# Masked attention over a tree, one core: three stores give their last partitions to SyncE's queue

## The chip, the core and the metric

The kernel runs on one core of a Trainium2 chip. The core has a matrix engine (TensorE, PE in the profile), a vector engine (VectorE, DVE), an activation engine (ScalarE, ACT), GpSimd (POOL) and SyncE (SP), which only issues transfers here. 16 DMA engines, which all queues share, move data between the DRAM and the on-chip memory of 128 partitions. POOL, SP and ACT each have a DMA queue of their own. The metric is the device time of one execution in microseconds (us), the median of several runs; less is better.

## The reference

Q, K and V have 8 x 12 = 96 heads of 512 rows of 64 floats. Row i may look at itself and at its ancestors in a binary tree.

```
mask[i, i] = 1;  parent = i
while parent > 0:
    parent = (parent - 1) // 2
    mask[i, parent] = 1
...
scores = einsum('bhqd,bhkd->bhqk', Q, K) / sqrt(64) + (1 - mask) * (-1e9)
weights = exp(scores - max);  weights = weights / (sum + 1e-10)
out = einsum('bhqk,bhkd->bhqd', weights, V)     # float32, [8, 12, 512, 64]
```

## The kernel before

The heads are taken in 48 pairs, and in twelve groups of eight heads (four pairs, `GP = 4`). The work of a pair has three parts. `T` transposes keys and queries on PE and copies them out of PSUM on DVE. `S` computes two score tiles on PE (lines 489 to 541), the mask as a product of codes that is added to them, and their exponentials on ACT. `V` multiplies with the values on PE (line 552), and `norm` (line 575) takes the reciprocal of the sums on DVE (line 585) and multiplies by it (line 590). The loop at line 767 runs `S T V` for each pair.

Loads are issued by POOL, in groups of eight heads, K, Q and V, and turn float32 into bf16 on the way. POOL also copies values and keys into the layouts that PE reads (lines 306 and 324). What POOL does stands in an order written out by hand, the string `POOL` (line 612): `k`, `q`, `v` are loads, `K`, `Q`, `t`, `c` are copies, `s0` to `s10` are the stores of eight heads, `p44` and `p45` stores of a pair. A word is emitted when `ready` (line 648) allows it; a store `s` of group g waits until pair 4 (g + 1) is due.

The results of groups 0 to 10 are written by `norm` into ten tiles `of` of 128 partitions x 8 heads x 256 floats, 1 MB each; a partition holds 8 x 1 KB of a tile, 8 KB. `of` of group 10 takes the buffer of group 0; the other groups have a buffer to themselves. `store` (line 597) issues one DMA of a whole tile on POOL's queue. The last four pairs have tiles `ol` of 256 KB and are stored by `store_pair` (line 604): pairs 44 and 45 by POOL, pair 46 by SP, pair 47 in two halves by SP and ACT. SP does nothing else from the first microseconds until pair 46 is done.

In the string, `s0` stands behind the last V load, `s1` behind the last K and Q loads, `s2` to `s4` among the copies for the last groups, and from `s5` on nothing but stores is left:

```
"k72 q72 K7 Q7 v80 k80 q80 t4.0 K8 v88 s0 Q8 k88 q88 t4.8 s1 K9 Q9 t5.0 s2 K10 s3 Q10 t5.8 s4 K11 Q11 s5 s6 s7 s8 s9 s10 p44 p45 "
```

Of the kernel before, what the change touches and what calls it, by code (L numbers as in the profile page):

```python
# [11 lines left out]
CODE_ROWS = 40  # L12
CODE_BITS = 16
NOUT = 10
COARSE = range(1, 12)
COARSE_K = range(1, 12)
BESIDE = {"K": range(3, 12), "Q": range(3, 12)}
# [104 lines left out]
def kernel(  # L122
# [7 lines left out]
    nc = tc.nc  # L130
    B, H, S, D = Q.shape
    P = nc.NUM_PARTITIONS
# [5 lines left out]
    KB, VB = 8, 16  # L138
# [13 lines left out]
    Or = out.rearrange("b h (p t) d -> p (b h) (t d)", t=4)  # L152
# [14 lines left out]
    small = ctx.enter_context(tc.tile_pool(name="small", bufs=4))  # L167
    opool = ctx.enter_context(tc.tile_pool(name="opool", bufs=NOUT))
    olast = ctx.enter_context(tc.tile_pool(name="olast", bufs=GP))
# [61 lines left out]
    def head(i, a):  # L231

        g, x = divmod(i, GP)
        return KB * g + GP * a + x if g in COARSE else 2 * i + a

# [13 lines left out]
    qTs, kTs, kqps, obs, ets, ofs = {}, {}, {}, {}, {}, {}  # L249
# [12 lines left out]
    def load_coarse(kept, name, src, h0, n):  # L262

        assert n == KB
        issued.update((name, h) for h in range(h0, h0 + n))
        to = kept[h0 // KB] = loads.tile([P, 2, 16, D], bf16, name=name)
        return nc.gpsimd.dma_start(
            out=to[:, :, :, :].rearrange("p g s d -> p g (s d)"),
            in_=src[32 * h0:32 * (h0 + n), :].rearrange("(g r) c -> r g c", g=2),
        )  # L270
# [6 lines left out]
    def load_q(h0, n):  # L277
        if h0 // KB in COARSE:
            return load_coarse(qsts, "qst", Qc, h0, n)
        return load(qsts, loads, "qst", KB, Qr, h0, n)  # L280
# [29 lines left out]
    def lay_beside(copy, name, g):  # L310
# [4 lines left out]
        src = kept[:, :, :, :].bitcast(mybir.dt.uint32)  # L315
        if g not in COARSE:
            src = src.rearrange("p (x a) t w -> p x t a w", a=2)
        elif name == "Q" or g in COARSE_K:
            src = src.rearrange("p a s w -> p s a w")
        else:  # L320
            src = src.rearrange("p (a x) t w -> p (x t) a w", a=2)
        if g in COARSE:
            dst = dst.rearrange("p x t a w -> p (x t) a w")
# [53 lines left out]
    def transpose_coarse(i):  # L377

        g, x = divmod(i, GP)
        kqps[i] = kqps[i - 1] if x == 3 else psT.tile([P, 2, 32, 32], bf16, name="kqp")  # L380
        if x < 2 and g in COARSE_K:
            assert all(("kst", h) in issued for h in range(KB * g, KB * g + KB))
            return transpose_rows(i, x)
        if x < 2:
            for half in range(2):
                transpose_keys(GP * g + 2 * x + half, kqps[i], half)
            return
        assert all(("qst", h) in issued for h in range(KB * g, KB * g + KB))
        for half in range(2):
            for y, t in enumerate(ORDER):  # L390
                four = 2 * x - 4 + half
                for rows, src in turned(
                    "Q", g, t, lambda b: b[:, four, t, :, :], lambda a: qsts[g][:, a, 4 * four + t, :]
                ):
                    u = 16 * half + y
                    dst = kqps[i][rows, x - 2, u:u + 13:4, :]
                    nc.tensor.transpose(out=dst, in_=src, identity=eye[:, 0:128])  # L397

    def transpose(i, halves=(0, 1)):
        g = i // GP  # L400
        if g in COARSE:
            return transpose_coarse(i)
# [18 lines left out]
    def evac(i):  # L421
# [5 lines left out]
        if g in COARSE_K:  # L427
            dst = kqgs[g][:, 1, 2 * (x % 2):2 * (x % 2) + 2, :, :]
        elif g in COARSE:
            dst = kqgs[g][:, 2 * (x % 2):2 * (x % 2) + 2, x // 2, :, :]  # L430
# [164 lines left out]
            )  # L595

    def store(eng, g):
        return eng.dma_start(  # L598
            out=Or[:, KB * g:KB * g + KB, :],
            in_=ofs[g][:, :, :, :].rearrange("p h t d -> p h (t d)"),  # L600
        )


    def store_pair(eng, i, a=0, n=2):
# [14 lines left out]
    def pool_program():  # L619

        ops = []
        for word in POOL.split():
            kind, *n = word[0], *(int(x) for x in word[1:].split(".") if x)
            if kind in "kqv":
                h0, size = n if len(n) == 2 else (n[0], KB)
                ops.append(({"k": load_k, "q": load_q, "v": load_v}[kind], h0, size))
            elif kind in "KQ":
                ops.append((lay_early if kind == "K" else lay_q, n[0]))
            elif kind == "c":
                o, part, h0, h1 = n  # L630
                ops.append((spread, nc.gpsimd.tensor_copy, o, part, h0, h1))
            elif kind == "t":
                o, h0 = n
                ops += [
                    (spread, nc.gpsimd.tensor_copy, o, part, h0, h0 + KB)
                    for part in (6, 7, 8, 9) + ((), (4, 5))[min(o, 1)]
                ]
            elif kind == "s":
                ops.append((store, nc.gpsimd, n[0]))
            elif kind == "p":  # L640
                ops.append((store_pair, nc.gpsimd, n[0]))
            elif kind == "e":
                ops.append((eye_order,))
            else:
                ops.append((code_order, n[0]))
        return ops
# [162 lines left out]
```

## Time and profile before

| what | value |
|---|---|
| median of 3 runs | 132.43 us (131.93 to 133.2) |
| the profiled execution | 132.84 us |
| its span, first to last instruction | 130.8 us |
| mean granted clock of TensorE | 0.986 |
| busy: PE, DVE, ACT, POOL | 88%, 73%, 76%, 74% |
| read from and written to DRAM | 37.86 MB, 12.58 MB |

The page gives busy times by engine, a strip of 40 equal slices of the span in which a digit is the busy share in tenths, the DMA queues (q0 is POOL's, q1 SP's, q10 ACT's, q8 and q14 fetch instructions) and the chain of work that ended last. A DMA share of 1.0 or more means that the packets of all 16 DMA engines cover the time; they overlap a little. The GB/s count bytes as they are written, so a load that halves its data counts half.

### The profile page before, as it was taken

Reading aid. Unit: us, or ns where it says so; the run is one execution under the profiler, and the core shown is the slowest. Engines: PE = TensorE matmul, PEld = TensorE weight load, DVE = VectorE, ACT = ScalarE, POOL = GpSimd, SP = SyncE. Lnnn points to the kernel's source line nnn. Section 1 sums busy time; section 2 is a strip of 40 time slices with the busy share of each in tenths; the row PEclk is TensorE's granted clock in tenths of the full one; section 3 lists DMA queues with packets and bytes.
Section 4 is the critical chain, followed back from the end, with each engine's and each line's share of the span. In section 5 each row is a group of like instructions: output and inputs, shape, how many; then the busy total and the mean of one; then the engine's idle time right before and its main releaser. Section 6 shows DMA issues by size and latency. Waiting matters only on the chain.

```text
span 130.8 us, 4949 instructions
## 1 busy us (share of the span) xinstructions
PE 115.4 (88%) x2132; PEld 82.6 (63%) x2133; DVE 95.9 (73%) x179; ACT 99.0 (76%) x160; POOL 96.3 (74%) x149
## 2 busy tenths in 40 slices
PE   4989996999998998995999997989989999989930
PEld 1444565776866676774776875767767777856620
DVE  4236778758958959774989798798998898775460
ACT  4339553787988988886778886887897897899920
POOL 6979978239899999999999999999996930202300
PEclk9999999999999999999999999999999999999995
DMA  4999999999999999999999999999999999999992
GB/s 124 195 185 205 209 185 211 201 211 205 210 197 217 201 206 202 209 205 207 212 199 211 202 209 207 205 210 232 336 220 357 406 401 401 401 402 401 384 352 94
DMA packets 24533, 32.13 MB, mean 246 GB/s; under 512 B 944, under 2 KB 15920, under 8 KB 24512
## 3 DMA queue, kind: packets, MB, share of 16 engines
q0 software_dynamic: 23232, 30.67, 110.9%
q1 hardware_dynamic: 720, 0.70, 1.7%
q10 hardware_dynamic: 560, 0.46, 1.0%
q8 instruction: 16, 0.26, 0.7%
q14 instruction: 5, 0.04, 0.1%
HBM read 37.86 MB, written 12.58 MB: 385 GB/s over the span
## 4 chain that ended last, share of the span: by engine, by line
PE 59%; DVE 25%; POOL 6%; issue 3%; ACT 3%; ACTq 0%; POOLq 0%
PE ob L552 16%; DVE kq L436 7%; PE s L494 7%; DVE of L590 7%; PE kqp L375 7%; PE s L499 6%; PE kqp L397 6%; PE s L519 5%; DVE vt L306 5%; PE s L525 5%; PE s L718 3%; POOL vt L306 3%; PE ob L718 2%; PE kqp L350 2%; DVE rec L585 2%
## 5 line engine op out<-in xcount | busy, mean ns | idle before, releaser
L510 ACT ACTIVATE e<-s 128x1024 bf16<-128x1024 f32 x48 | 49.1, 1023 | 21.3 <-PE s L499 20.9
L306 POOL COPY vt<-vst 32x256 uint32<-32x256 uint32 (+2 forms) x70 | 34.9, 499 | 8.9 <-DMA vst<-in_V_dram 5.7
L541 ACT ACTIVATE e<-s 128x384 bf16<-128x384 f32 (+1 forms) x92 | 41.4, 505 | 0.0
L552 PE MATMUL ob<-vt,e 128*128 128x65 bf16 (+1 forms) x940 | 36.9, 197 | 2.4 <-DVE of L590 2.1
L552 PEld LDWEIGHTS <-e 128*128 128x128 bf16 (+1 forms) x960 | 31.2, 102 | 7.9 <-DVE of L590 3.7
L590 DVE TENSOR_TENSOR of<-ob,rec 128x512 f32<-128x512 f32 x44 | 30.4, 691 | 1.5
L306 DVE COPY vt<-vst 32x512 uint32<-32x512 uint32 (+1 forms) x33 | 20.6, 625 | 1.0
L499 PE MATMUL s<-kq 64*128 64x512 bf16 x96 | 18.4, 379 | 2.1 <-DVE kq L436 2.1
L525 PEld LDWEIGHTS <-kq 64*128 64x128 bf16 x384 | 16.3, 110 | 6.3
L598 POOL DMA_DIRECT2D out_dram<-of x11 | 9.8, 897 | 13.5 <-DVE of L590 13.5
L585 DVE RECIPROCAL rec<-ob 128x8 f32<-128x8 f32 x47 | 9.6, 204 | 12.8 <-PE ob L552 12.5
L444 DVE COPY kq<-kqp 128x1024 bf16<-128x1024 bf16 x22 | 15.1, 687 | 4.9 <-PE kqp L375 4.4
L525 PE MATMUL s<-kq 64*128 64x160 bf16 (+1 forms) x384 | 17.9, 210 | 0.0
L494 PE MATMUL s<-qcoarse,codes 40*128 40x512 bf16 x88 | 17.2, 387 | 0.0
L519 PE MATMUL s<-qcoarse,codes 40*128 40x480 bf16 x88 | 16.3, 364 | 0.3
L436 DVE COPY kq<-kqp 128x2048 bf16<-128x2048 bf16 x11 | 13.5, 1224 | 2.2 <-PE kqp L397 1.8
L375 PE MATMUL kqp<-mixed,Kbeside 128*128 128x128 bf16 x144 | 11.1, 220 | 2.8 <-POOL Kbeside L324 1.7
L519 PEld LDWEIGHTS <-codes 40*128 40x128 bf16 x96 | 7.6, 95 | 8.4 <-issue 2.0
L306 ACT COPY vt<-vst 32x512 uint32<-32x512 uint32 (+1 forms) x17 | 10.7, 627 | 1.7 <-DMA vst<-in_V_dram 1.3
L397 PE MATMUL kqp<-ptile,Qbeside 128*128 128x128 bf16 x144 | 11.2, 220 | 0.2 <-DVE kq L444 0.2
L375 PEld LDWEIGHTS <-Kbeside 128*128 128x128 bf16 x144 | 8.3, 98 | 4.2 <-POOL Kbeside L324 2.0
L257 POOL DMA_DIRECT2D vst<-in_V_dram x12 | 10.9, 910 | 0.0
(45 smaller groups left out, 102.2 us busy)
## 6 DMA issues: line engine op xcount, KB each, us to landing
out_dram<-of POOLq DMA_DIRECT2D x11, 1024.0 KB, 15.6
vst<-in_V_dram POOLq DMA_DIRECT2D x12, 512.0 KB, 14.0
kst<-in_K_dram POOLq DMA_DIRECT2D x11, 512.0 KB, 11.9
qst<-in_Q_dram POOLq DMA_DIRECT2D x11, 512.0 KB, 12.3
out_dram<-ol POOLq DMA_DIRECT2D x2, 256.0 KB, 5.3
qst<-in_Q_dram POOLq DMA_DIRECT2D x3, 128.0 KB, 7.1
ol<-in_K_dram SPq DMA_DIRECT2D x1, 256.0 KB, 2.9
ol<-in_Q_dram ACTq DMA_DIRECT2D x1, 256.0 KB, 3.2
```

The source lines that it names most:

```text
L306: return copy(out=dst, in_=src)
L375: nc.tensor.transpose(out=dst, in_=src, identity=perm)
L397: nc.tensor.transpose(out=dst, in_=src, identity=eye[:, 0:128])
L436: return nc.vector.tensor_copy(out=dst, in_=src) if x == 3 else None
L494: nc.tensor.matmul(out=columns(g, sp[:, a, :], 0, 512), lhsT=k1code[64 * a:64 * a + CODE_ROWS, :], rhs=query_codes(i, a, 0, 0, 512), start ...
L499: nc.tensor.matmul(out=columns(g, sp[:, a, :], 0, 512), lhsT=keys(i, a, TOP), rhs=queries(i, a, 0, 512), start=False, stop=True,)
L510: nc.scalar.activation(out=dst, in_=src, func=AF.Exp, scale=scale)
L519: nc.tensor.matmul(out=columns(g, flat[:, a, :], 32, 512), lhsT=k2code[64 * a:64 * a + CODE_ROWS, :], rhs=query_codes(i, a, 1, 32, 512), s ...
L525: nc.tensor.matmul(out=columns(g, flat[:, a, :], lo, hi), lhsT=keys(i, a, TILE2[t]), rhs=queries(i, a, lo, hi), start=False, stop=t == 1,)
L541: nc.scalar.activation(out=dst, in_=src, func=AF.Exp, scale=scale)
L552: nc.tensor.matmul(out=ob[lo:hi, a, 65 * t:65 * t + 65], lhsT=e[:, a, PLACE[t], lo:hi], rhs=vt[:, head(i, a) % VB, tile_v, 0:D + 1], **flags,)
L590: nc.vector.tensor_tensor(out=dst, in0=o4[:, a:a + n, :, 0:D], in1=rec[:, a:a + n, :, :].to_broadcast([P, n, 4, D]), op=ALU.mult,)
```

## The change

`store` cuts the tile of three of the groups by partitions, by a table `SPLIT`. The first piece goes out on POOL's queue, where the whole tile went before; the other pieces go out on SP's queue.

```diff
+SPLIT = {1: (112, 120, 128), 4: (120, 124, 128), 7: (120, 122, 124, 126, 128)}
...
     def store(eng, g):
-        return eng.dma_start(
-            out=Or[:, KB * g:KB * g + KB, :],
-            in_=ofs[g][:, :, :, :].rearrange("p h t d -> p h (t d)"),
-        )
+        cuts = SPLIT.get(g, (P,))
+        for n, (lo, hi) in enumerate(zip((0,) + cuts, cuts)):
+            (nc.sync if n else eng).dma_start(
+                out=Or[lo:hi, KB * g:KB * g + KB, :],
+                in_=ofs[g][lo:hi, :, :, :].rearrange("p h t d -> p h (t d)"),
+            )
```

POOL stores 112 partitions of group 1 and 120 of groups 4 and 7. SP stores 2 x 8 partitions of group 1, 2 x 4 of group 4 and 4 x 2 of group 7. All other stores stay whole. The lines of the kernel move by one to three (`store` issues from line 601, `store_pair` from 610).

SP's program before, whole. `ol` is the tile of a pair, and a wait is given in brackets (DVE's is for the data, DMAHW's for an earlier DMA of SP or ACT that used the same semaphore):

```order
L804 UNCONDITIONAL_BRANCH [waits barrier_Pool_Activation_PE_DVE_SP_release]
L183 DMA ol<-in_K_dram 128x2x256
L191 DMA codes<-tree_codes 16x1280 [waits DVE_49]
L607 DMA out_dram<-ol 128x2x256 [waits DVE_49]
L607 DMA out_dram<-ol 128x256 [waits DVE_49]
L804 UNCONDITIONAL_BRANCH
```

And SP's program now, from the load of the codes to the last store. `of` is the tile of eight heads:

```order
L192 DMA codes<-tree_codes 16x1280 [waits DVE_49]
L601 DMA out_dram<-of 8x8x256 [waits DVE_49]
L601 DMA out_dram<-of 8x8x256
L601 DMA out_dram<-of 4x8x256 [waits DVE_49]
L601 DMA out_dram<-of 4x8x256
L601 DMA out_dram<-of 2x8x256 [waits DMAHW0_49,DVE_49]
L601 DMA out_dram<-of 2x8x256 [waits DMAHW1_49]
L601 DMA out_dram<-of 2x8x256 [waits DMAHW2_49]
L601 DMA out_dram<-of 2x8x256 [waits DMAHW3_49]
L610 DMA out_dram<-ol 128x2x256 [waits DMAHW4_49,DVE_49]
L610 DMA out_dram<-ol 128x256 [waits DMAHW5_49,DVE_49]
```

Eight DMAs have come in between; the first of each group waits for DVE, and none for POOL.

POOL's program before, at its end, from the copy of group 10's keys on:

```order
L324 COPY Kbeside<-kst 128x1024
L598 DMA out_dram<-of 128x8x256
L324 COPY Qbeside<-qst 128x1024
L306 COPY vt_118<-vst 32x8x32 x4
L306 COPY vt_118<-vst 64x8x2x32 x2
L598 DMA out_dram<-of 128x8x256
L324 COPY Kbeside<-kst 128x1024
L324 COPY Qbeside<-qst 128x1024
L598 DMA out_dram<-of 128x8x256 x6
L607 DMA out_dram<-ol 128x2x256 x2
```

And now:

```order
L325 COPY Kbeside<-kst 128x1024
L601 DMA out_dram<-of 128x8x256
L325 COPY Qbeside<-qst 128x1024
L307 COPY vt_118<-vst 32x8x32 x4
L307 COPY vt_118<-vst 64x8x2x32 x2
L601 DMA out_dram<-of 120x8x256
L325 COPY Kbeside<-kst 128x1024
L325 COPY Qbeside<-qst 128x1024
L601 DMA out_dram<-of 128x8x256 x2
L601 DMA out_dram<-of 120x8x256
L601 DMA out_dram<-of 128x8x256 x3
L610 DMA out_dram<-ol 128x2x256 x2
```

No step of POOL has moved; two of the stores shown (of groups 4 and 7), and that of group 1 further up, carry fewer partitions.

## The prediction

> **What bounds the kernel now.** I read the page first for the whole span, then the table by stage for its end, then the chain of waits, then the DMA view in short windows.
>
> ```profile
> span 130.8 us, 4949 instructions
> PE 115.4 (88%) x2132; PEld 82.6 (63%) x2133; DVE 95.9 (73%) x179; ACT 99.0 (76%) x160; POOL 96.3 (74%) x149
> DMA  4999999999999999999999999999999999999992
> q8 instruction: 16, 0.26, 0.7%
> HBM read 37.86 MB, written 12.58 MB: 385 GB/s over the span
> ```
>
> No compute engine is full, but the DMA engines are, in 38 of the 40 slices. The profiled run took 132.84 us, 2.0 more than its span and 0.41 above the median of the three runs (132.43); sums below are made against 132.84 and then moved down by 0.41.
>
> ```profile
> core 0: us, PE busy (x) PEld busy (x) DVE busy (x) ACT busy (x) POOL busy (x), PEclk, DMA share, GB/s
> 106.00:111.00 5.00, 4.96 (x90) 3.58 (x88) 4.43 (x10) 4.39 (x8) 0.00 (x0) 1.00 1.02 401
> 111.00:116.00 5.00, 4.63 (x94) 3.50 (x90) 4.01 (x8) 4.53 (x8) 0.89 (x1) 1.00 1.03 401
> 116.00:121.00 5.00, 4.65 (x92) 3.22 (x93) 2.55 (x7) 4.77 (x9) 0.89 (x1) 1.00 1.02 403
> 126.00:128.20 2.20, 0.00 (x0) 0.00 (x0) 0.80 (x3) 0.00 (x0) 0.00 (x0) 0.75 0.85 313
> 128.20:129.60 1.40, 0.00 (x0) 0.00 (x0) 0.00 (x0) 0.00 (x0) 0.00 (x0) 0.50 0.28 96
> 129.60:130.80 1.20, 0.00 (x0) 0.00 (x0) 0.00 (x0) 0.00 (x0) 0.00 (x0) 0.50 0.00 0
> ...
> 126.41 0.42 DVE ol L590
> ...
> 126.87 0.35 ACTq L607 DMA_DIRECT2D out_dram<-ol  x1
> ```
>
> From 106 us on only stores run (the last load is in by 101.2, a row below), at 401 to 403 GB/s. Compute ends at 126.83 (the last multiply), the last store is issued at 126.87, and then there are 2.7 us in which only DMA runs. The next line is the DMA share in steps of 50 ns from 128.0 to 130.0.
>
> ```profile
> DMA  9845444335344223332322223000010000000000
> ```
>
> At 128.0 nearly all 16 DMA engines work; from about 128.2 only 4 tenths, some 6 of 16; they stop one after another, and the last packets end at about 129.5. So the others had emptied their queues by 128.2, last store and all, and the end is set by the few that are behind. That tail, 129.55 - 128.2 = 1.35 us, is all that a better balance of stores can take away: the other engines' last work hangs on the store issued at 126.87, which compute sets.
>
> Why some lag: each fetch of instructions is one packet of 16 KB on one DMA engine.
>
> ```profile
> DMA packets 410, 1.59 MB, mean 398 GB/s; under 512 B 24, under 2 KB 24, under 8 KB 409
> q8 instruction: 1, 0.02, 1.6%
> ```
>
> That is the window 107 to 111: 1.6% of 16 engines over 4 us is 1.02 us of one engine. Sixteen such packets (page: 0.7% of 16 x 130.8 us, 14.6 us) make an average of 0.9 us on each engine; spread unevenly, they give lags of this size. The trace has no engine numbers, so it doesn't say which engines lag.
>
> **The change, part by part.** *Price of a row.* A store of 1 MB has 128 rows of 8 KB. At 401 GB/s it takes 1.049 MB / 401 = 2.61 us; with all 16 engines at work that is 8 rows on each, 0.33 us a row. The change moves 16 + 8 + 8 = 32 rows of 11 x 128, and removes no byte.
>
> *What POOL's three stores lose.* 112 rows are 7 for each of 16 engines. 120 don't divide by 16: 7.5 on average, or 8 on fifteen engines and none on one. For one engine the three together are 1 + 0.5 + 0.5 = 2 rows fewer on average, 1 row at the least, and 1 + 8 + 8 = 17 rows at the most.
>
> *What SyncE's eight DMAs add.* The trace has no DMA of fewer than 16 partitions, so it doesn't show where they land. Bounds, if no row is cut and the rows of one DMA go to different engines: none of the eight puts a row on a given lagging engine (0), or each does (8 rows). Net, for the engine that ends last: from -17 rows (then the next one behind ends last) over -2 and -1 to 8 - 1 = +7, that is from the end of the tail (-1.35 us) to +2.29 us. I take -1 row, -0.33 us. It is the nearest to what is sure: every engine loses a row of the 112-row store, and eight narrow DMAs reach only some of the 16, while about 6 of 16 are in the tail.
>
> [...]
>
> *POOL's issue time.* The 1 MB stores take 885 ns of POOL each, the 256 KB ones 716.
>
> ```profile
> L598 POOL DMA_DIRECT2D out_dram<-of x11: 885/885/963, 78.3 to 120.1; - x11
> DMA to landing us min/median/max: 7.2/15.6/19.3
> L607 POOL DMA_DIRECT2D out_dram<-ol x2: 707/716/725, 122.1 to 123.9; - x2
> ```
>
> Between 716 and 963 ns apiece, three of them change POOL by -0.5 to +0.2 us. It costs nothing: a store waits 7 to 19 us in the queue anyway. Were that cover gone, it would be those 0.2 us.
>
> *SyncE.* Eight issues of about 0.37 us are 3 us on a sequencer that waits 124.4 us:
>
> ```profile
> SPq L607 <- DVE rec L585: 124.4, 2, 124.0
> L607 SPq DMA_DIRECT2D out_dram<-ol x2: 350/370/389, 125.6 to 126.3; - x2
> 34.42 0.69 DVE L590 TENSOR_TENSOR of<-ob,rec 128x512 f32<-128x512 f32 x1
> 65.06 0.69 DVE L590 TENSOR_TENSOR of<-ob,rec 128x512 f32<-128x512 f32 x1
> 92.39 0.69 DVE L590 TENSOR_TENSOR of<-ob,rec 128x512 f32<-128x512 f32 x1
> ```
>
> SyncE waits for the data alone, not for POOL's turn: the multiplies of pairs 7, 19 and 31 (rows at 34.42, 65.06, 92.39) end at 35.1, 65.8 and 93.1 us, so the three groups start there, up to some 50 us ahead of POOL's parts. The waits on semaphores of earlier DMAs that SyncE's new stores and its two last ones have are for transfers that landed long before; even the last four, from 93.1 on, are done some 30 us ahead of 125.59. Cost 0.
>
> *Loads behind them.* The new stores share the DMA engines with loads. A load lands with its slowest engine, so it is late by at most 2 rows (0.65 us) after 35 and 66 us, and 4 rows (1.3 us) after 93. Who would wait:
>
> ```profile
> 101.23 1.04 POOL L324 COPY Qbeside<-qst 128x1024 uint32<-128x1024 uint32 x1 [1.12 <-DMA qst<-in_Q_dram]
> 102.22 3.52 POOL L598 DMA_DIRECT2D out_dram<-of  x4
> ...
> 106.83 0.57 PE kqp L375 x8
> 111.41 0.55 PE kqp L397 x8
> ```
>
> The last Q load is the only one waited for after 40 us (1.12). If it is 1.3 us later still, its copy ends at 103.6, before the transposes at 111.4 read it, and the four stores behind it go out by 107; a store lands a median of 15.6 us after its issue, so those issued earlier still fill the queue. Hidden; with the cover gone it would be 1.3 us.
>
> *Sum.* 132.84 - 0.33 = 132.5, and against the median 132.43 - 0.33 = 132.1 us.
>
> **Rivals.**
> 1. *The whole tail goes.* If the narrow stores fall on engines that are ahead and the 120-row stores spare the worst laggard, all end near 128.2: 132.43 - 1.35 = 131.1. Against it: some 6 engines lag, by up to 1.35 us, or 4 rows; one spared engine leaves five, which lose a row or two. For it: the last two steps of the share line are one engine alone (128.2 + 1.0 to 1.35).
> 2. *The slower side: a laggard receives rows.* One mechanism: rows of narrow DMAs gather on a few engines, and one of these is in the tail already. Each row is 0.33 us at the very end, since that engine never rests before it. It decides from 2 rows on: +0.65, and +2.29 at 7 rows, 133.1 to 134.7. For it: DMAs of four and of two rows can't reach more than four and two engines, and 6 of 16 lag; if those two are always the same, one of them is in the tail with a chance of about 6 in 10 were lag a matter of luck. Against it: the lag isn't luck if the fetches go to fixed engines, and the narrow stores may be on others.
> 3. *Nothing changes.* The rows are spread evenly again, 2 more on each engine for 2 fewer: 132.4. [...] For it: 401 GB/s in all store windows, whatever is sent. Against it: two, four or eight rows can't lie evenly on 16 engines unless rows are cut.
>
> [...]
>
> **How the numbers follow.** Forecast, -0.33 us (132.1): 0.40; its own range is -0.65 to 0, 131.8 to 132.4. Rival 1 (131.1): 0.13. Rival 2 (133.1 to 134.7): 0.35. Rival 3 (132.4): 0.12. The range 131.0 to 134.3 holds the floor and most of rival 2. A measurement of this kernel can tell about 1%, 1.3 us, from no change. Faster by over that is rival 1 alone: 0.13. Slower by over it is rival 2 from 4 rows on, 0.27 of its 0.35; within 1% are the rest, 0.40 + 0.12 + 0.08 = 0.60.
>
> **What the profile after would show.** Right: the last issue still at about 126.9, store windows near 400 GB/s, SyncE's narrow stores at 35, 66 and 93 us, and a tail after 128.2 that is shorter by 0.3 us. Rival 1: a share line that falls at once. Rival 2: a tail of one or two engines, share 0 or 1 in the line, that goes on beyond 129.6 by a third of a microsecond a row. Rival 3: the tail as it is. I would be wrong in another way if the last issue moved from 126.87: then a load that came late held up compute.

## The result and the profile after

The changed kernel took 138.5 us (median of 4 runs, 138.12 to 141.82) against 132.81 us for the kernel before (4 runs): a ratio of 1.044, with a 95% interval of 1.035 to 1.054. Here and below a ratio leaves out the runs that took over 1.5% longer than the fastest of the same kernel, while a median takes all of them, so the two need not agree. The forecast was 132.1 us with a range of 131.0 to 134.3: the sign was wrong, and the time lies outside the range. The profiled execution took 138.16 us.

First the page, lines that answer to those shown of before: the span, the slices of TensorE's clock, of the DMA share and of GB/s.

```profile
span 136.4 us, 4962 instructions
...
PEclk9999999999999999999999999999999999779975
DMA  4999999999999999999999999999999999995970
GB/s 142 169 177 205 209 202 212 200 213 200 207 213 216 200 209 203 210 202 212 201 214 209 207 208 204 212 221 341 221 356 398 374 356 364 334 345 192 366 281 23
...
HBM read 37.86 MB, written 12.58 MB: 370 GB/s over the span
```

The bytes are the same. The span is 5.6 us longer, and the strips show three new things in the last quarter, where only stores run: GB/s between 334 and 398 where before had 401 to 403, a clock of 0.7 in two slices, and a slice of DMA share 0.5. The table by stage takes them apart (columns as in the prediction: PE, PEld, DVE, ACT, POOL busy, clock, DMA share, GB/s).

```profile
106.00:111.00 5.00, 4.96 (x101) 3.67 (x100) 4.38 (x8) 4.76 (x10) 0.44 (x1) 1.00 1.02 366
113.00:115.00 2.00, 0.00 (x0) 0.00 (x0) 0.00 (x0) 0.66 (x2) 0.41 (x1) 1.00 1.05 377
117.00:119.00 2.00, 2.00 (x34) 1.74 (x30) 1.58 (x3) 1.74 (x3) 0.00 (x0) 0.68 1.00 338
119.00:121.00 2.00, 2.00 (x24) 1.06 (x22) 1.46 (x3) 1.20 (x3) 0.00 (x0) 0.50 1.01 363
123.00:125.00 2.00, 1.88 (x38) 1.25 (x38) 1.20 (x3) 1.97 (x4) 0.03 (x1) 1.00 0.60 213
125.00:127.00 2.00, 2.00 (x44) 1.39 (x43) 0.90 (x2) 1.83 (x4) 0.93 (x2) 1.00 0.45 182
133.00:135.00 2.00, 0.00 (x0) 0.00 (x0) 0.00 (x0) 0.00 (x0) 0.00 (x0) 0.50 0.11 38
```

*Slower transfers at the same share.* From 106 to 111 the 16 DMA engines are as busy as before (1.02), but carry 366 GB/s, not 401. So they aren't idle: each packet takes longer. The DMA view of 107 to 111 us, which the prediction showed of before with 410 packets, says so in packets (of the second row: packets, MB, share):

```profile
DMA packets 378, 1.45 MB, mean 364 GB/s; under 512 B 23, under 2 KB 23, under 8 KB 378
...
q0 software_dynamic: 378, 1.45, 102.1%
```

The records of single packets (which no view lists) tell which. In before a packet of 4 KB of a store takes 165 ns, and 9 of the 2,129 that start between 102 and 124 us take over 240. In after it is 157 of 1,901, with a median of 316 ns; 137 of them start from 106 to 113 us or from 115.6 to 124, and these are the times in which the cut stores of groups 4 and 7 move.

*A late fetch of instructions.* The fetch that before shows in 107 to 111 (the row of q8 there) is missing in the view above. It comes in 113 to 115:

```profile
q8 instruction: 1, 0.02, 2.9%
```

By its record it starts at 113.52, 5.15 us later than before's 108.37, and takes 0.9 us. In the chain of waits PE stands still until 1.6 us after its end:

```profile
112.18 0.55 PE kqp L398 x8
112.89 3.10 issue
115.99 0.63 PE ob L553 x15
116.62 0.32 PE s L495 x2
```

"issue" means that PE waits for nothing that the profile shows, no semaphore and no engine. That it has no instructions is a reading of this: PE stops after five of a run of 20 multiplies of `V`. Before has no such piece. PE's clock then falls to 0.68 and 0.50 (rows 117 to 121 above), and the others wait. The table of waits from 100 us on (wait in total, times, longest):

```profile
POOL out_dram L601 <- DVE of L591: 17.6, 2, 11.6
...
ACT e L511 <- PE s L500: 7.0, 9, 3.6
...
PE ob L553 <- issue: 3.1, 1, 3.1
```

POOL's store of group 10 is the one that waits 11.6 us; it goes out at 124.97 instead of 120.10, and meanwhile the DMA queue runs dry (213 and 182 GB/s in the rows from 123 to 127).

*The end.* POOL's and ACT's last issues:

```profile
124.97 0.89 POOL L601 DMA_DIRECT2D out_dram<-of  x1 [11.56 <-DVE of L591]
```

```profile
131.73 0.35 ACTq L610 DMA_DIRECT2D out_dram<-ol  x1
```

The last multiply ends at 131.70 (before 126.83), the last store lands at 135.43 by its completion record (before 129.93). The 5.5 us between the two kernels' last landings are, by the starts of the multiplies (line 591; before line 590) of single pairs:

| part | us |
|---|---|
| multiplies are late by, from pair 10 (43 us) to pair 39 (111.5 us) | 0.8 |
| pair 39 to pair 40: PE's standstill | 3.3 |
| pair 40 to pair 42: the low clock | 0.8 |
| last multiply to last landing, 3.1 to 3.7 | 0.6 |

The first row is no finding: kernels without any sign of harm (e7, e14 below) end their compute 0.8 and 0.6 us later than before's profiled run too.

### The profile page after: what moved, and what is told of

It reads as the page before. It is cut to its first block, busy times and chain, and to the rows that moved or that the text cites. A ratio compares the mean times of both kernels' runs of the same rounds, so it can differ in the third digit from the quotient of the medians.

```text
span 136.4 us, 4962 instructions
## 1 busy us (share of the span) xinstructions
PE 116.2 (85%) x2132; PEld 83.1 (61%) x2133; DVE 96.6 (71%) x179; ACT 99.0 (73%) x160; POOL 97.0 (71%) x149
## 4 chain that ended last, share of the span: by engine, by line
PE 46%; DVE 18%; POOL 11%; DMA 10%; issue 6%; ACT 4%; POOLq 0%; ACTq 0%
PE ob L553 14%; DMA kst<-in_K_dram 10%; PE s L495 6%; PE kqp L398 5%; PE kqp L376 5%; PE s L500 5%; DVE of L591 5%; DVE kq L437 4%; PE s L520 4%; POOL vt L307 4%; DVE vt L307 4%; PE s L526 4%; PE s L721 3%; POOL Kbeside L325 2%; ACT e L511 2%
## 5 line engine op out<-in xcount | busy, mean ns | idle before, releaser
L553 PE MATMUL ob<-vt,e 128*128 128x65 bf16 (+1 forms) x940 | 37.6, 198 | 5.1 <-issue 3.1
L553 PEld LDWEIGHTS <-e 128*128 128x128 bf16 (+1 forms) x960 | 31.7, 103 | 10.8 <-issue 3.4
## 6 DMA issues: line engine op xcount, KB each, us to landing
qst<-in_Q_dram POOLq DMA_DIRECT2D x3, 128.0 KB, 7.8
```

Of the source, the lines that this page charges most:

```text
L553: nc.tensor.matmul(out=ob[lo:hi, a, 65 * t:65 * t + 65], lhsT=e[:, a, PLACE[t], lo:hi], rhs=vt[:, head(i, a) % VB, tile_v, 0:D + 1], **flags,)
```

## Experiments

All are timed against the kernel before in the same job (medians there 133.09 to 133.62 us). "Slow" counts packets of 4 KB over 240 ns that start from 102 to 124 us, of about 2,000; "fetch" is the start of the fetch that before has at 108.37, the 14th of 16 in every run; "gap" is a standstill of PE over 0.9 us after 100; "tail" runs from the end of the last multiply to the last landing. The last four columns are of the profiled run of each.

| run | what is cut | median, us (n) | ratio, 95% interval | slow | fetch | gap | tail |
|---|---|---|---|---|---|---|---|
| before | nothing | 132.81 (4) | | 9 | 108.37 | - | 3.1 |
| after | 1, 4, 7 | 138.5 (4) | 1.044, 1.035 to 1.054 | 157 | 113.52 | 3.1 | 3.7 |
| e1 | 1 at 112 | 134.3 (10) | 1.002, 0.998 to 1.007 | 10 | 108.67 | - | 2.3 |
| e2 | 4 at 120 | 135.56 (5) | 1.019, 1.012 to 1.026 | 35 | 114.58 | 3.6 | 1.7 |
| e3 | 7 at 120 | 136.22 (4) | none | 33 | 109.61 | - | 2.0 |
| e4 | 1, 4, 7 at 112 | 141.77 (4) | 1.063, 1.056 to 1.071 | 189 | 108.41 | - | 10.2 |
| e5 | 4 at 112 | 136.5 (4) | 1.014, 1.003 to 1.025 | 57 | 108.36 | - | 5.4 |
| e6 | 4 at 120, no SyncE | 135.34 (10) | 1.003, 0.997 to 1.009 | 45 | 109.12 | - | 3.6 |
| e7 | SyncE's eight alone | 134.93 (4) | none | 8 | 110.0 | - | 3.4 |
| e8 | 1 at 120 | 134.34 (10) | 1.005, 1.001 to 1.009 | 8 | 108.64 | - | 2.2 |
| e9 | 4 at 120, in 1's place | 134.21 (10) | 1.004, 0.999 to 1.008 | 22 | 109.08 | - | 3.4 |
| e10 | 1 at 120, in 4's place | 136.29 (4) | 1.019, 1.009 to 1.028 | 58 | 113.55 | 1.2 | 3.9 |
| e11 | 2 at 120 | 135.26 (10) | 1.015, 1.011 to 1.020 | 35 | 108.58 | - | 4.2 |
| e12 | 3 at 120 | 135.84 (4) | 1.019, 1.011 to 1.027 | 82 | 110.52 | - | 6.3 |
| e13 | 4 as 64 + 64, POOL | 135.35 (4) | 1.015, 1.009 to 1.022 | 26 | 109.47 | - | 4.4 |
| e14 | 4 by heads, POOL | 133.34 (10) | 1.001, 0.997 to 1.005 | 9 | 108.47 | - | 2.9 |
| e15 | 1 as 64 + 64, POOL | 133.83 (10) | 1.000, 0.996 to 1.005 | 12 | 109.45 | - | 4.3 |
| e16 | the change again | 141.46 (1) | none | 245 | 111.76 | 1.6 | 8.5 |
| e17 | all at 120, no SyncE | 134.76 (1) | none | 158 | 108.08 | - | 5.8 |
| e18 | all as 64 + 64, POOL | 136.93 (5) | 1.023, 1.012 to 1.034 | 162 | 112.30 | - | 3.9 |

A median moves with what happens in single runs; e2's profiled run took 138.16 us, e10's 138.02, e12's 136.81 and e18's 139.84, each the longest of its kernel; e8's, 132.86, was the shortest of its ten, and e3's, 133.69, the shortest of its four (the others 136.04 to 136.66).

### Which of the three stores costs: e1 to e4

Each group alone, and all three cut at 112. The line that goes is the same in the later edits of `SPLIT` too.

```diff
-SPLIT = {1: (112, 120, 128), 4: (120, 124, 128), 7: (120, 122, 124, 126, 128)}
+SPLIT = {1: (112, 120, 128)}
```

> Group 1 alone is split (POOL 112 partitions, SP 8 + 8); groups 4 and 7 are whole. Theory P (it is the 120-row stores on POOL's queue: 120 rows don't lie on the 16 DMA engines as 128 or 112 do, packets of 4 KB take 300 to 600 ns in place of 165, and PE's instruction fetch is held up): no such packets, no gap of PE over 1 us after 100 us, time within 1% of before. Theory R (narrow DMAs gather rows on a few DMA engines that lag, rival 2 on record): one row at most on a lagging engine, 0.33 us, also within 1%. Theory S (whatever goes out on SP's queue beside POOL's holds up the fetch): slower by about a third of the change's 4.4%, 1.5%.

```diff
+SPLIT = {4: (120, 124, 128)}
```

> Group 4 alone is split (POOL 120 partitions, SP 4 + 4). Theory P: slow packets from the time this store is moved (about 106 us), the fetch of PE that falls due at about 109 us is late, PE stands still for some 3 us there, time 3 to 4% above before. Theory R: two rows at most on a lagging engine, 0.65 us, 0.5%. Theory S: about a third of the change, 1.5%, and no slow packets that begin with this store.

```diff
+SPLIT = {7: (120, 122, 124, 126, 128)}
```

> Group 7 alone is split (POOL 120 partitions, SP 2 + 2 + 2 + 2). Theory P: slow packets from about 114 us on, later than the fetch due at 108; the time depends on whether the fetches due at 115 and 122 are held up, 1 to 3% above before. [...] Theory S: about a third or more of the change, since it has four of the eight SP DMAs, 1.5 to 2.2%.

```diff
+SPLIT = {1: (112, 120, 128), 4: (112, 116, 120, 124, 128), 7: (112, 114, 116, 118, 120, 122, 124, 126, 128)}
```

> All three groups are split at 112 partitions; SP stores the last 16 of each, in DMAs of 8 (group 1), 4 (group 4) and 2 (group 7), 14 DMAs in place of 8. [...] Theory R: slower than the change itself by 4 more rows, 1.3 us, all in the tail. Theory S: slower than the change, with the gap of PE still there, since SP moves 48 rows in place of 32.

Group 1 alone costs nothing that can be told from zero (1.002). Group 4 alone costs 1.9%. For group 7 the cost isn't settled: three of its four runs are 2.2 to 2.6% above the median of before (133.15), the profiled one is 0.4% above it, and there is no interval. So the runs don't show how the 4.4% divide. Group 4 alone shows the standstill of PE too; e2's fetch starts at 114.58, and its table of waits has the same row as that of after:

```profile
PE ob L553 <- issue: 3.6, 1, 3.6
```

Cutting at 112 everywhere, so that no store has 120 partitions, doesn't help but hurts most (6.3%), and without a standstill. There the loss lies in the end, in e4's table by stage after the last multiply at 128.2:

```profile
106.00:111.00 5.00, 4.85 (x100) 3.72 (x98) 4.48 (x9) 4.65 (x9) 2.77 (x4) 1.00 1.01 343
...
131.00:134.00 3.00, 0.00 (x0) 0.00 (x0) 0.00 (x0) 0.00 (x0) 0.00 (x0) 0.50 0.23 88
134.00:137.00 3.00, 0.00 (x0) 0.00 (x0) 0.00 (x0) 0.00 (x0) 0.00 (x0) 0.50 0.09 32
137.00:139.70 2.70, 0.00 (x0) 0.00 (x0) 0.00 (x0) 0.00 (x0) 0.00 (x0) 0.50 0.02 8
```

A share of 0.23, then 0.09 of 16 is four engines, then one or two, that go on alone for over 6 us. So beside slow packets (343 GB/s at a share of 1.01) the end of the run comes late in two ways: engines that fall behind, or a fetch that comes late. In e4 a part of the first may be the rows that SyncE's 14 DMAs add, up to 3.6 us by an estimate (one row of each on the same engine, less one of each of POOL's three stores of 112 partitions: 11 rows of 0.33 us), of a tail that is 7.1 us longer than in before; the two aren't separated. Nor do the runs show what decides between the ways: e12 below has 82 slow packets and a fetch 2.2 us later than in before, e2 has 35 and a fetch 6.2 us later. That 120 partitions, or the engine that they leave out, is what hurts falls with e4.

### Which part of a cut: e5 to e8

```diff
+SPLIT = {4: (112, 120, 128)}
```

> Group 4 is split as group 1 was: POOL 112 partitions, SP 8 + 8; the rest is whole. Theory P (a POOL store of 120 rows, not one of 112, makes the packets slow and the fetch late): no packets of 4 KB over 240 ns but the few around fetches, no gap of PE over 1 us after 100 us, time within 1% of before. Theory Q (any cut POOL store in the stage of stores alone does it, 112 or 120; group 1 escaped because loads ran beside it): slow packets from about 106 us and a late fetch, time as with group 4 at 120, about 2% above before.

```diff
+SPLIT = {4: (120,)}
```

> POOL stores 120 partitions of group 4 and nobody stores the last 8 (8 x 8 KB of the output are left out); SP has no new DMA. Theory P: the same slow packets from about 106 us, a late fetch and a gap of PE near 113 us as with SP's two DMAs, time about 2% above before. Theory N (SP's narrow DMAs do it, by the rows they gather or by their queue): nothing of it, time at or below before (64 KB less to move, at most 0.2 us).

```diff
     def store(eng, g):
+        eng.dma_start(
+            out=Or[:, KB * g:KB * g + KB, :],
+            in_=ofs[g][:, :, :, :].rearrange("p h t d -> p h (t d)"),
+        )
         cuts = SPLIT.get(g, (P,))
         for n, (lo, hi) in enumerate(zip((0,) + cuts, cuts)):
-            (nc.sync if n else eng).dma_start(
-                out=Or[lo:hi, KB * g:KB * g + KB, :],
+            if n:
+                nc.sync.dma_start(
+                    out=spare[lo:hi, KB * g:KB * g + KB, :],
...
```

> All POOL stores are whole, and SP issues the change's eight narrow DMAs at the same points, but into a spare tensor in DRAM, 256 KB on top of the work. [...] Theory N: the gap of PE near 113 us and the slow packets are there, 3% or more above before.

```diff
+SPLIT = {1: (120, 124, 128)}
```

> Group 1 is split at 120 (POOL 120 partitions, SP 4 + 4), groups 4 and 7 are whole. Theory P: where the split at 112 cost nothing, 120 costs: slow packets from about 99 us while this store moves, and the fetch of PE due at about 102 us is late by more than 1 us, with a gap of PE near 106 us; time 1 to 3% above before. Theory Q: the store moves partly beside loads, so nothing happens, within 1% of before.

Group 4 at 112 costs 1.4% too, with 57 slow packets (e5): theory P falls, and what theory Q says of a cut at 112 or 120 among stores holds. The slow packets belong to POOL's cut store: with it and without any DMA of SyncE there are 45 (e6), with SyncE's eight DMAs beside whole stores 8, as in before (9). e6's time doesn't settle whether they cost anything without SyncE's DMAs: its ratio of 1.003 rests on four of its ten runs, and the median of all ten is 1.4% above that of before (135.34 against 133.52). In its profiled run, 134.46 us, the slow packets neither delayed the fetch nor left one engine far behind, so they needn't be lost time in every run. That a cut on POOL's queue costs time with no DMA on SyncE is shown by e13 below. e7's time has no interval; its runs of 133.18 and 134.13 and of 135.73 and 135.97 don't settle whether 256 KB more to write cost something. Its packets are clean:

```profile
q0 software_dynamic: 412, 1.59, 101.1%
q8 instruction: 1, 0.02, 1.5%
```

And group 1 costs hardly more at 120 (e8: 0.5%, with 8 slow packets), so it isn't 112 that spared it in e1. "Harmless" here and below means within 1% of before.

### The group or its place: e9 to e12

In e9 and e10, `s1` and `s4` change places in POOL's order, and the cut falls on 4 or on 1.

```diff
+SPLIT = {4: (120, 124, 128)}
-... K8 v88 s0 Q8 k88 q88 t4.8 s1 K9 Q9 t5.0 s2 K10 s3 Q10 t5.8 s4 K11 Q11 ...
+... K8 v88 s0 Q8 k88 q88 t4.8 s4 K9 Q9 t5.0 s2 K10 s3 Q10 t5.8 s1 K11 Q11 ...
```

> Group 4 alone is split at 120 (SP 4 + 4), and groups 4 and 1 change places in POOL's order: group 4 is stored where group 1 stood, behind the last loads. Theory A (it is the group: where its tile and its output lie): slow packets while it moves, from about 98 us. Theory B (it is the place in the queue: a cut store is harmless while loads are beside it, harmful among whole stores): no packets of 4 KB over 240 ns but those around fetches, no gap of PE after 100 us, time within 1% of before.

```diff
+SPLIT = {1: (120, 124, 128)}
-... t4.8 s1 K9 Q9 t5.0 s2 K10 s3 Q10 t5.8 s4 K11 Q11 ...
+... t4.8 s4 K9 Q9 t5.0 s2 K10 s3 Q10 t5.8 s1 K11 Q11 ...
```

> The other half of the crossing: group 1 alone is split at 120 (SP 4 + 4) and is stored where group 4 stood. Theory A: no slow packets, as with group 1 in its old place, within 1% of before. Theory B: slow packets from about 106 us, some engines 2 us further behind, 1 to 2% above before, with a gap of PE if the fetch due at 109 is caught.

```diff
+SPLIT = {2: (120, 124, 128)}
```

> Group 2 alone is split at 120 (SP 4 + 4); it is the next in the queue behind group 1 and moves at about 101 to 106 us, when the last loads have just landed. Theory B: some slow packets from 102 us on, fewer than with group 4; time 0 to 2% above before. Theory A: whether it is slow says nothing of the place.

```diff
+SPLIT = {3: (120, 124, 128)}
```

> Group 3 alone is split at 120 (SP 4 + 4); it moves at about 104 to 109 us among whole stores only. Theory B: slow packets from about 104 us, as with group 4, and 1 to 2% above before. Theory A: no prediction from the place; clean, if the group decides and group 3 is like group 1.

The place decides. Group 4 in group 1's place is harmless (1.004, though with 22 slow packets), group 1 in group 4's place costs 1.9%. The profiled run of e10 lands its last store 4.8 us later than before's; 2.6 us of that are there by pair 10 already, before any cut store of POOL moves, and 1.3 us come at pair 40, with a fetch at 113.55 and a standstill of 1.15 us in its timeline of PE:

```profile
115.89 0.64 PE L553 MATMUL ob<-vt,e 128*128 128x65 bf16 x15 [1.15 <-issue]
```

Groups 2 and 3, which stand behind group 1 in the queue and move when the last loads are in, cost 1.5% and 1.9%. e12's DMA view of 107 to 111 us shows the slow packets at their plainest, 353 where before had 409 in the same 4 us at the same share:

```profile
q0 software_dynamic: 353, 1.36, 99.9%
```

### Partitions or pieces: e13 to e16

From the kernel before, with no DMA on SyncE: group 4 as two DMAs of 64 partitions (e13), or as two DMAs of all 128 partitions and four heads each (e14); group 1 as two of 64 (e15). And the change once more (e16).

```diff
+        for lo in (0, 64) if g == 4 else ():
+            eng.dma_start(
+                out=Or[lo:lo + 64, KB * g:KB * g + KB, :],
...
```

> Group 4 is stored by POOL in two DMAs of 64 partitions each (0 to 63, 64 to 127), nothing on SP. [...] Theory U (a DMA that leaves an engine out or gives it another number of rows upsets the balance, and lag does the rest): 64 rows are 4 for each engine twice, the same bytes each, so no slow packets, within 1% of before.

```diff
+        for lo in (0, 4) if g == 4 else ():
+            eng.dma_start(
+                out=Or[:, KB * g + lo:KB * g + lo + 4, :],
...
```

> Group 4 is stored by POOL in two DMAs of all 128 partitions and four heads each. [...]

```diff
+        for lo in (0, 64) if g == 1 else ():
...
```

> The 64 + 64 cut for group 1, whose store moves at 98 to 103 us, behind the last loads. [...] Within 1.5% of before. Theory B alone (the place decides whatever the cut): no slow packets at all.

> The changed kernel once more, for its trace alone. If the gap of PE is what the late fetch costs, it is there again: no matmul for about 3 us near 113 us, the fetch due at 109 us served 3 to 5 us late. If the gap is absent and the time is still about 138 us, the lag of the DMA engines alone makes the time, in the tail.

Two halves by heads cost nothing (1.001, 9 slow), two halves by partitions 1.5%. Both send the same bytes in the same number of DMAs, and 16 divides the rows of each, so neither one DMA more nor rows that don't divide by 16 are needed for the loss: the cut by partitions is. Theory U falls by this. The slow packets are few: e13's two DMAs move 1 MB, which is 256 packets of 4 KB, and 26 are slow from 102 to 124 us. In e14's view of 107 to 111 us the rate is that of before:

```profile
DMA packets 429, 1.61 MB, mean 403 GB/s; under 512 B 38, under 2 KB 38, under 8 KB 428
```

e15 repeats that group 1's place is harmless. e16 shows both ways of the loss in one run: the fetch at 111.76 with a standstill of 1.6 us, and a tail of 8.5 us.

### Beside whole stores, or by itself: e17 and e18

> All eleven stores of eight heads are issued by POOL for 120 partitions; their last 8 partitions are stored by nobody (704 KB of the output left out), SyncE issues none of it. Measured by the packets of 4 KB that take over 240 ns between 104 and 120 us (37 in the run with group 4 alone, some 600 packets of this size go by in these 16 us), not by the time, since bytes are missing. [...] Theory C (a cut store is slow by itself): slow ones through the whole stretch, over 200. [...]

```diff
+SPLIT = {g: (120,) for g in range(11)}
```

> All eleven stores of eight heads go as two stores of 64 partitions, both on POOL's queue; all bytes are stored. With group 4 alone cut so, the time was 1.0154 of before and some 20 packets of 4 KB took over 240 ns. Theory M (cut beside whole is what costs): no change, 0.995 to 1.008, and fewer than 20 slow packets between 104 and 120 us. Theory C (each cut store costs by itself): seven or eight cuts among stores alone, 1.5% each if they add, so 1.05 to 1.12, and over 100 slow packets.

```diff
+        for lo in (0, 64):
+            eng.dma_start(
+                out=Or[lo:lo + 64, KB * g:KB * g + KB, :],
...
```

Theory M falls: with no whole store of eight heads anywhere, slow packets go on through the whole stretch (105 in e17 and 134 in e18 from 104 to 120 us). Theory C has the direction but not the size. e18 has the over 100 slow packets that it asked for, e17 doesn't have over 200 (of 1,411 packets in that stretch, not of the 600 that its expectation reckoned with), and 2.3% for e18 is not 5% or more.

Nor can e18's 2.3% be put down to slow packets. In its profiled run the multiplies are 1.1 us late at pair 29 and from 5.7 to 6.4 us late from pair 31 (98.8 us) to the end: the stretch with the slow packets adds nothing to that, and the tail only 0.8 us. Most of the lateness comes from POOL, which now issues two DMAs for each store (1.41 us in place of 0.90) and waits 1.99 and 0.95 us for earlier loads to land before it issues more. Its copy of the keys starts at 91.64 us (before 85.74), and PE waits for it. From the timelines of POOL and PE:

```profile
85.16 0.72 POOL L267 DMA_DIRECT2D qst<-in_Q_dram  x1 [1.99 <-DMA qst<-in_Q_dram]
...
92.74 1.03 PE L375 MATMUL kqp<-mixed,Kbeside 128*128 128x128 bf16 x8 [2.98 <-POOL Kbeside L324]
```

What e18's other four runs lose their time to is not known.

For the rate of a cut store, though, e18 holds the cleanest piece of evidence of all. Its store of group 10 is issued late, when the queue has run nearly dry, so that all engines start on the first half of 64 partitions within 0.4 us and nothing else moves. Timeline of POOL, and the DMA view of 127.5 to 129.4 us:

```profile
126.20 1.37 POOL L599 DMA_DIRECT2D out_dram<-of  x2 [7.01 <-DVE of L590]
```

```profile
DMA packets 101, 0.41 MB, mean 216 GB/s; under 512 B 1, under 2 KB 1, under 8 KB 101
...
q0 software_dynamic: 101, 0.41, 100.3%
```

All 16 engines are busy, and they carry 216 GB/s, about half of 401. From 126.6 to 127.4 us only one engine had been at work, and its packets took 165 ns each; from 127.5 on the packets slow down, and from 128.0 to 129.4 nearly all take 313 ns. So here a store of 64 partitions that moves alone has about half the rate of the whole stores in before.

## Why the prediction was wrong

**The step that failed** is "What POOL's three stores lose". It priced the pieces that POOL keeps by their number of rows alone, 1 to 17 fewer on one engine at 0.33 us, with the 401 GB/s of the whole store for each row. No rival had another rate; rival 3 even took "401 GB/s in all store windows, whatever is sent" as a row in its favour, but all those windows hold stores of 128 partitions only. In the place of that step the runs showed that while a store cut by partitions moves among stores, some packets take about 300 ns in place of 165 (a median of 316 in after): 9 slow packets become 33 to 82 with one group cut at 112 or 120 (e2, e3, e5, e6, e10 to e12), and after carried 366 GB/s from 106 to 111 us. The same step left out what waits for the DMA engines: of the 5.5 us between the last landings, 3.3 and 0.8 us are PE's standstill and the low clock behind it.

How far the rate falls is shown for one case, and why it falls isn't shown. Shown: a store of 64 partitions on which all 16 engines work at once has about half the rate (e18: 216 GB/s and 313 ns a packet; the whole stores in before: 401 GB/s and 165 ns). The records don't say which partitions an engine reads, so what makes a packet of a cut store slow stays open, for 112 and 120 as for 64. Nor do the runs part the reading from the writing: a store of 64 partitions also writes other rows in DRAM than a whole one, and no run cuts the one without the other.

**"Cost 0" for the narrow DMAs.** The trace now shows where their rows go: the landings of SyncE's eight come in eight, four and two steps (those of the first from 40.20 to 41.42 us), so here a DMA of eight, four or two rows ran on as many engines, as the prediction's bounds assumed. They went out at 35.6, 66.6 and 93.9 us, near the 35, 66 and 93 that were said; the row of all eight runs from the first to the end of the last:

```profile
35.64 59.40 SPq L601 DMA_DIRECT2D out_dram<-of  x8
```

They add no slow packets (8 in e7, 9 in before). Rival 2, rows on a laggard, gave a time above before's, but by another mechanism than the one that acted: POOL's stores without SyncE's rows have the slow packets as well (e6). Its tail of engines that go on alone did come, in e4, e12 and e16, but longer than any count of rows gives: 10.2 us in e4.

**"The tail is all that a balance can take".** This was right as a bound of the gain. In the profiled runs of e1 and e8 the tail is 2.3 and 2.2 us instead of 3.1, as a better balance would make it; but e2 and e3 have 1.7 and 2.0, and these are single runs, so the balance isn't shown. The ratios show no gain (1.002 and 1.005).

**"The last issue still at about 126.9."** It moved to 131.73, which the prediction named as the sign of another error, with a late load as the cause. The sign was right and the cause was not: no load was late, a fetch of instructions was. The prediction had the fetches in its account, but only as a reason for lags of the DMA engines, not as a transfer that PE waits for. That a late fetch stops PE rests on four profiled runs in which both appear (after, e2, e10, e16: fetch between 111.76 and 114.58, standstill from 1.15 to 3.63 us). In all four PE stops after five of 20 multiplies of `V` of the same pair and goes on 1.4 to 1.6 us after the end of the fetch, and against PE's own lateness at pair 39 the fetch is 2.5 to 4.9 us late. In the others PE doesn't stop there, and by the same measure the fetch is at most 1.2 us late (e12; in e18 it starts at 112.30, but PE is 6.1 us behind). It was not tried by itself. Why the fetch starts 3.4 to 6.2 us later than in before is open.

**"401 GB/s"** as the price of a byte holds for stores that cover all 128 partitions (e14: 403). It held for the cut of group 1 too: e1 carries 393 to 403 GB/s from 100 to 106 us, before 391 to 416. Why a cut in that place does no harm is open. Of the runs with one store cut by partitions, the harmless ones with whole bytes (e1, e8, e9, e15) are those whose cut store begins to move beside the last loads. But the loads alone don't explain it: in e1 the last packet of a load starts at 100.5 us, and by its completion records the cut store lands from 100.2 to 103.3.

## What to carry to other kernels

When transfers are the bound, check what a cut does to the partitions that a transfer covers before counting its rows: halve a transfer along its free size, with all 128 partitions in each piece, and the rate stayed here (403 GB/s in e14, 398 in before, from 107 to 111 us), halve it by partitions and it dropped to about half in one case (216 GB/s in e18). Look for fewer packets at the same DMA share; a full share doesn't say that the engines work at their rate (1.02 in before and after, at 401 and 366 GB/s). The DMA engines also carry the instructions (16 fetches of 16 KB here), so a change to transfers can show up as an engine that waits for "issue" (PE, 3.1 us in after).

## What the runs showed that was not expected

- A packet of 4 KB of a store takes 165 ns in before, where its DMA covers 128 partitions, and 313 ns in e18 when it covers 64 and nothing else moves.
- The store of 120 partitions of group 4 in after seems to leave one engine without rows: 16 packets of 16 bytes follow one another from 105.93 to 106.23 us, and the first of the store's 16 landings (106.67 us) comes 1.9 us ahead of the second (108.57). There are 32 such packets in after, with two stores of 120 partitions, 176 in e17 with eleven, and none in before.
- A fetch of 16 KB takes 0.89 to 1.04 us of one DMA engine in before, 0.89 to 1.26 in after. Beside stores the 14th was served up to 6.2 us later than in before (114.58 in e2 against 108.37), and PE stood still for 3.6 us, with its clock at 0.68 and 0.50 behind the standstill in after.
